# A hybrid attention, convolution and SwiGLU block: the order of the attention values' split, when V is copied, and where the last block's transposed products are read

## The chip, the cores and the metric

The kernel runs on one core of one Trainium2 chip. The metric is the device time of one execution in microseconds (us), the median of several runs. The profile is one further execution, recorded by the hardware profiler.

## The reference

One layer on x of 256 rows and 2048 columns, in float32, cut to what matters here:

```python
xn = rms_norm(h, norm1_g)
proj = xn @ w_in                                   # 2048 x 5120
q, k, v, ga, gg = split(proj)                      # 4 heads; q, k: 2 x 128 each, v: 256 each
att = diff_attention(rope(rms_norm(q)), rope(rms_norm(k)), v, lam)
att = rms_norm(att, subln_g) * (1 - lambda_init)   # over a head's 256 columns
u = silu(layer_norm(causal_depthwise_conv(ga * sigmoid(gg))))
h = h + concatenate([att, u]) @ w_out
hn = rms_norm(h, norm2_g)
h = h + (silu(hn @ w_gate) * (hn @ w_up)) @ w_down # 5632 hidden columns
```

In diff_attention each head has two score matrices; the weights are the first softmax less lam times the second.

## The kernel before, in words

**Products.** Every float32 product is made of three faster ones. A matrix is split into a rounded part (hi) and the residue (lo), and hi times hi, lo times hi and hi times lo are summed in PSUM. Weights come from HBM in chunks of two 128-row pieces of 512 columns (raw, L329); ScalarE rounds them (whi, L338), VectorE subtracts (wlo, L347). For some chunks ScalarE negates the raw chunk instead (lod, L333, or wlo, L341) and GpSimd's queue issues a DMA that adds the weights on top (L334, L342). The rounding runs three chunks ahead of the product before the FFN, four in it. The left operands are split in the same way and transposed: the pairs are called lhi and llo, and mahi and malo for attention heads 0 and 1.

**Order of the work.** Everything is written out by hand in one program order, engine by engine; what one engine needs of another becomes a wait on a semaphore. The main line is run_chunks (L470): for each chunk it issues loads, roundings and subtractions ahead, then the chunk's matmuls (multiply, L359). A chunk has a first half (hi times weights hi, L377, and lo times weights hi, L378) and a second half (hi times weights lo, L383). After each half multiply calls resume() (L250), which advances every side job by one step. Side jobs are Python generators: each issues some instructions and then yields; lag(n) yields n times, so that the job goes on n steps later. A step is thus half a chunk. In the FFN the same goes for units of a block (multiply_pair, multiply_two). Side jobs run in the order in which they were started.

**PSUM.** Of eight banks four are accumulators (acc) and four are shared by side jobs (aux). room(n) lets a job wait, while the program is written out, until fewer than five are held; a new tile takes a bank that earlier jobs have released in program order, and its first instruction waits until the last reader of that bank is done. Accesses to one bank by two engines are put in program order by waits.

**Attention.** For two heads at a time: attend_scores (L719) makes scores (ps_s, L728), masks and finds the maximum (L736, L738), takes exponentials (L747), reciprocals (L756), the product a with minus lam on GpSimd (L758), p (L767) and the weights (L774), transposes them (ps_wt, L780 to L782) and copies them to qT (L785). V comes from two blocks of w_in; when one has been multiplied, v_done (L788) copies it to SBUF with the row scale (L791) and starts attend_values (L797) for its two heads. That job multiplies (ps_o, L807), sums squares (L513 through L812), makes the scale on GpSimd (L216, L217), scales (att, L818), transposes (ps_at, L826), and splits the transposed tile into hi and lo (split_scaled, L236: L239 on ScalarE, L240 on VectorE), once for each half e of the head's columns. The pairs are columns 2*hd and 2*hd+1 of the left operand of w_out.

**Meanwhile.** VectorE works off the convolution's taps (y, L593), handed out between the halves of chunks by a credit. conv_back (L607) transposes the result (ps_y, L614), copies it (L619), takes the layer norm (L624, L633, L642), transposes back (ps_ln, L652) and applies Silu (L656). The chunks of w_out follow those of V: columns 0 to 3 of the left operand for three blocks n, then 4 and 5, then 6 and 7, then the convolution's.

**FFN.** The 5632 hidden columns are eleven blocks of 512, in groups of 4, 4 and 3. After a group, its part of w_down is multiplied. From the second block on, a part of the products is made by a scheme of seven products in place of eight (pair_sums, PRODUCTS; units "s"), the rest plainly (units "g" and "u"; L1106, L1107, L1111). block_done (L1201) combines a block's sums in tiles sum0 to sum3, and five steps later transposed (L936) takes the result in two halves t: transposes to PSUM (ps_a, L917), rounds (L948) and, three steps later, subtracts (L950). Where a half goes into the seven-product scheme, pair_forms (L954) is used, which first copies the PSUM tile to SBUF (L960). During a block all accumulators and three aux banks hold sums, so one bank is left for ps_a. For the last block, j = 10, both halves take the plain way.

Of the kernel before, what the change touches and what calls it, by code (L numbers as in the profile page):

```python
# [13 lines left out]
F32 = mybir.dt.float32  # L14
F32R = mybir.dt.float32r
AF = mybir.ActivationFunctionType
ALU = mybir.AluOpType
AX = mybir.AxisListType

P = 128  # L20
D = 2048
S = 256
# [8 lines left out]
FF = 5632  # L31
KD = D // P
N = 512
# [79 lines left out]
def tile_block(  # L113
# [6 lines left out]
    act, dve, pool, pe, sp = nc.scalar, nc.vector, nc.gpsimd, nc.tensor, nc.sync  # L120
# [6 lines left out]
    pre = prestack.enter_context(tc.tile_pool(name="pre", bufs=2))  # L127
# [37 lines left out]
    def col(key, k):  # L165
        return cols[:, AT[key] + k : AT[key] + k + 1]
# [45 lines left out]
    def rsqrt_mean(dst, ss, n, eps):  # L212

        k = dst.shape[-1]
        t = small.tile([P, 8], F32, tag="rsq", name="rsq")
        pool.tensor_scalar(t[:, :k], ss, 1.0 / n, eps, ALU.mult, ALU.add)  # L216
        pool.tensor_tensor(dst, t[:, :k], neghalf[:, :k], ALU.pow)  # L217
# [5 lines left out]
    def lhs_pair(pfx, k):  # L223
        if k % 2 == 0:
            halves[pfx] = lhs_two(pfx, k)
        return tuple(t[:, k % 2, :] for t in halves[pfx])

    def lhs_two(pfx, k):
        at = slot[0] % (KD // 2) * 4
        slot[0] += 1  # L230
        return arena_two(at)
# [4 lines left out]
    def split_scaled(pair, src, scale):  # L236

        hi, lo = pair
        act.activation(hi, src, AF.Copy, scale=scale)  # L239
        dve.scalar_tensor_tensor(lo, src, scale, hi.bitcast(F32), ALU.mult, ALU.subtract)  # L240
# [6 lines left out]
    def start(gen):  # L247
        running.append(gen)
# [6 lines left out]
    def lag(n):  # L255
        for _ in range(n):
            yield
# [4 lines left out]
    def room(n, hold=0):  # L262
        while held[0] + n > AUX:
            yield
        held[0] += hold
# [6 lines left out]
    def spend(us):  # L272
        credit[0] -= us
# [237 lines left out]
    def square_sum(src, accum, **kw):  # L511
        junk = pre.tile([P, N], F32, tag="junk", name="junk", bufs=1)
        act.activation(junk[:, : src.shape[-1]], src, AF.Square, accum_out=accum, **kw)  # L513
# [91 lines left out]
    mixa = {}  # L605
# [180 lines left out]
        wTs[hd] = wT  # L786

    def v_done(b, ps):  # L788
        yield
        for m in range(NM):  # L790
            act.activation(v_sb[m][:, b * N : (b + 1) * N], ps[m], AF.Copy, scale=rstd1[m])  # L791
        yield
        for hd in (2 * b, 2 * b + 1):
            start(attend_values(hd))
            yield

    def attend_values(hd):  # L797
        while hd not in wTs:
            yield
        wT = wTs.pop(hd)  # L800
        yield from lag(2)
        atts = []
        yield from room(1, 1)
        o = aux_ps.tile([P, NM, E], F32, tag="aux", name="ps_o")
        for m in range(NM):
            for k in range(m + 1):
                pe.matmul(o[:, m, :], wT[:, (0 if m == 0 else 1 + k), :], v_sb[k][:, hd * E : (hd + 1) * E],  # L807
                          start=k == 0, stop=k == m)
        yield
        ss = small.tile([P, NM], F32, tag="sso", name="sso")  # L810
        for m in range(NM):
            square_sum(o[:, m, :], ss[:, m : m + 1])  # L812
        r = small.tile([P, NM], F32, tag="ro", name="ro")
        rsqrt_mean(r, ss, E, EPS)
        yield from lag(2)
        for m in range(NM):
            at_ = pre.tile([P, E], F32, tag="att", name="att", bufs=4)
            act.activation(at_, o[:, m, :], AF.Copy, scale=r[:, m : m + 1])  # L818
            atts.append(at_)
        held[0] -= 1  # L820
        yield
        yield from room(1)
        pt = aux_ps.tile([P, 2, S], F32, tag="aux", name="ps_at")
        for e in range(2):
            for m in range(NM):
                pe.transpose(pt[:, e, m * P : (m + 1) * P], atts[m][:, e * P : (e + 1) * P], ident)  # L826
        for e in range(2):
            mixa[2 * hd + e] = lhs_pair("a", 2 * hd + e) if hd >= 2 else tuple(
                pre.tile([P, S], F32R, tag=t, name=t, bufs=4) for t in ("mahi", "malo"))
            split_scaled(mixa[2 * hd + e], pt[:, e, :], col("sg", e))  # L830
        spend(-0.9)


# [48 lines left out]
    ffn = {}  # L882
# [30 lines left out]
    def transpose_two(pt, aa, t):  # L913
        for i in range(2):
            for m in range(NM):
                c = (2 * t + i) * P
                pe.transpose(pt[:, i, m * P : (m + 1) * P], aa[m][:, c : c + P], ident)  # L917

    def group_of(j):
        return next((g for g in range(len(FGROUPS)) if j < sum(FGROUPS[: g + 1])), None)  # L920

    def place(g):

        pairs = DOWN[g]["pairs"]
        at = 7 * len(pairs)
        fhi, flo = (a[:, :at].rearrange("p (f q) c -> p f q c", f=7) for a in arena)
        twos = [(j, t) for j in range(sum(FGROUPS[:g]), sum(FGROUPS[: g + 1])) for t in range(2) if (j, t) not in pairs]
        free = [arena_two(i) for i in range(at, BLOCKS - 3, 4)]
        free += [tuple(a[:, i] for a in spare_lhs) for i in range(2)]
        assert len(free) >= len(twos)  # L930
        down[g] = dict(forms=(fhi, flo), pairs=pairs, twos=twos, at=dict(zip(twos, free)), ready=set())
# [4 lines left out]
    def transposed(j, aa):  # L936
        g = group_of(j)
        if g not in down:
            place(g)
        d = down[g]  # L940
        for t in range(N // P // 2):
            pt = aux_ps.tile([P, 2, S], F32, tag="aux", name="ps_a")
            transpose_two(pt, aa, t)
            if (j, t) in d["pairs"]:
                yield from pair_forms(j, t, pt)
            else:
                hi, lo = d["at"][j, t]
                act.copy(hi, pt)  # L948
                yield from lag(3)
                dve.tensor_tensor(lo, pt, hi.bitcast(F32), ALU.subtract)  # L950
            d["ready"].add((j, t))
            yield from lag(2)

    def pair_forms(j, t, pt):  # L954

        fp = ffn["pool"]
        q = down[group_of(j)]["pairs"].index((j, t))
        fhi, flo = (f[:, :, q] for f in down[group_of(j)]["forms"])
        a = fp.tile([P, 2, NM, P], F32, tag="sum0", name="af")
        act.copy(a, pt)  # L960
        a11, a21, a12, a22 = a[:, 0, 0], a[:, 0, 1], a[:, 1, 0], a[:, 1, 1]
        act.copy(fhi[:, :2], a[:, :, 0])
        act.activation(fhi[:, 2], a22, AF.Copy, scale=-1.0)
        yield from lag(2)
        f = fp.tile([P, 4, P], F32, tag="sum2", name="fs")
        dve.scalar_tensor_tensor(f[:, 1], a21, -1.0, a22, ALU.mult, ALU.subtract)
        dve.scalar_tensor_tensor(f[:, 2], f[:, 1], -1.0, a11, ALU.mult, ALU.subtract)
        dve.tensor_tensor(f[:, 3], a11, a21, ALU.subtract)
        dve.tensor_tensor(f[:, 0], a12, f[:, 2], ALU.subtract)
        dve.tensor_tensor(flo[:, :2], a[:, :, 0], fhi[:, :2].bitcast(F32), ALU.subtract)  # L970
        dve.scalar_tensor_tensor(flo[:, 2], a22, -1.0, fhi[:, 2].bitcast(F32), ALU.mult, ALU.subtract)
        yield from lag(2)
        act.copy(fhi[:, 3:], f)
        yield from lag(2)
        dve.tensor_tensor(flo[:, 3:], f, fhi[:, 3:].bitcast(F32), ALU.subtract)
# [225 lines left out]
    def block_done(j, q):  # L1201
        while "g" not in halfway:
            yield
        g, u = halfway.pop("g"), halfway.pop("u")
        for m, i in enumerate((Q3, QX)):
            dve.tensor_tensor(u[m], q[i], u[m], ALU.add)
        for m in range(NM):
            dve.tensor_tensor(u[m], u[m], g[m], ALU.mult)
        yield from lag(TO_TRANSPOSE)
        yield from transposed(j, u)  # L1210
# [51 lines left out]
    for b in range(2):  # L1262
        block("w_in", VC + b * N, range(KD), fx, lambda ps, b=b: v_done(b, ps))
# [66 lines left out]
```

## Time and profile before

| | us |
|---|---|
| median of 3 runs | 1044.78 |
| lowest and highest | 1044.53, 1044.81 |
| the profiled execution | 1043.19 |
| its span, first to last instruction | 1041.0 |
| TensorE busy | 1030.0 |
| VectorE busy | 864.5 |
| ScalarE busy | 685.1 |
| GpSimd busy | 157.4 |

The profiled execution's own time is 2.2 us more than its span, and 1.6 us less than the median. The granted TensorE clock was full throughout. The profile calls the engines PE (TensorE's matmuls; PEld its weight loads), DVE (VectorE), ACT (ScalarE), POOL (GpSimd) and SP. A row of the timeline gives start and duration in us, engine, line, operation, output and inputs, shape and count; idle time of the engine just before it stands in brackets, with what ended it. Matmuls overlap, so a row's duration is longer than the distance to the next matmul.

### The profile page before, as it was taken

What the parts mean: (1) busy time and instruction counts of PE and PEld (TensorE: products, weight loads), DVE (VectorE), ACT (ScalarE), POOL (GpSimd) and SP (SyncE); (2) the same over time, 40 slices, a digit from 0 to 9 for tenths busy, and PEclk for the clock granted to TensorE, in tenths of its full rate; (3) what the DMA queues carried; (4) which work ended last, traced back from release to release, by engine and by line L of the source; (5) the groups of instructions that cost most, each with busy time, mean ns of one, the idle gap of its engine ahead of it and who ended that gap; (6) DMA issues with size and microseconds to landing.
All of it is one profiled execution on the core that took longest, in us unless ns stands there. A gap on an engine that the chain in (4) does not pass through costs nothing.

```text
span 1041.0 us, 13235 instructions
## 1 busy us (share of the span) xinstructions
PE 1030.0 (99%) x4739; PEld 854.7 (82%) x4739; DVE 864.5 (83%) x1088; ACT 685.1 (66%) x865; POOL 157.4 (15%) x197
## 2 busy tenths in 40 slices
PE   8999999999999999999999999999999999999998
PEld 8888888887788888788888888888888888888786
DVE  5799989996546599999979689998896697998983
ACT  6855567857756567777656567776765666767661
POOL 0130134322110101011002120110101121001121
PEclk9999999999999999999999999999999999999999
DMA  9776867675566669898889998987979999889896
GB/s 361 277 205 227 258 184 205 197 206 155 188 182 233 227 217 284 232 328 241 260 238 294 269 308 265 306 236 245 303 201 270 306 272 327 236 249 301 241 252 134
DMA packets 65346, 258.06 MB, mean 248 GB/s; under 512 B 7424, under 2 KB 8448, under 8 KB 57856
## 3 DMA queue, kind: packets, MB, share of 16 engines
q1 hardware_dynamic: 48224, 201.34, 53.4%
q0 software_dynamic: 16768, 55.58, 28.0%
q8 instruction: 37, 0.61, 0.2%
q10 hardware_dynamic: 288, 0.29, 0.1%
q14 instruction: 29, 0.24, 0.1%
HBM read 248.80 MB, written 8.39 MB: 247 GB/s over the span
## 4 chain that ended last, share of the span: by engine, by line
PE 94%; ACT 2%; DVE 1%; issue 1%; DMA 1%; POOL 1%; SPq 0%; DVEq 0%; ACTq 0%
PE q L1106 11%; PE q L1107 11%; PE q L1111 11%; PE acc L383 11%; PE acc L378 11%; PE acc L377 11%; PE q L1085 9%; PE q L1087 8%; PE q L1086 8%; PE ps_a L917 1%; DMA raw<-in_wts_dram 1%; ACT whi L338 1%; PE ps_s L728 1%; PE ps_h L854 0%; PE ps_qk L713 0%
## 5 line engine op out<-in xcount | busy, mean ns | idle before, releaser
L338 ACT CAST whi<-raw 128x1024 fp32r<-128x1024 f32 (+1 forms) x261 | 270.7, 1045 | 105.7 <-PE acc L378 46.3
L347 DVE TENSOR_TENSOR wlo<-raw,whi 128x1024 fp32r<-128x1024 f32 (+1 forms) x173 | 209.4, 1216 | 76.5 <-ACT whi L338 76.5
L377 PE MATMUL acc<-whi,lhi 128*128 128x512 f32 (+1 forms) x448 | 167.4, 379 | 1.6 <-ACT whi L338 1.2
L378 PE MATMUL acc<-whi,llo 128*128 128x512 f32 (+1 forms) x448 | 165.7, 375 | 0.9 <-DVE llo L240 0.9
L1068 DVE TENSOR_TENSOR wl<-wt,wh 128x2048 fp32r<-128x2048 f32 x58 | 132.6, 2287 | 20.1 <-ACT wh L1063 20.1
L1059 ACT CAST wh<-wb 128x1536 fp32r<-128x1536 f32 x58 | 86.0, 1483 | 87.1 <-PE q L1086 42.8
L342 POOL DMA_DIRECT2D wlo<-in_wts_dram x74 | 65.0, 889 | 510.7 <-ACT wlo L341 482.6
L1106 PE MATMUL q<-whi,chi 128*128 128x512 f32 x320 | 124.7, 390 | 0.0
L1107 PE MATMUL q<-whi,clo 128*128 128x512 f32 x320 | 124.6, 389 | 0.0
L1063 ACT CAST wh<-wt 128x2048 fp32r<-128x2048 f32 x58 | 110.4, 1904 | 18.6 <-DVE wt L1054 18.6
L1085 PE MATMUL q<-wh,fhi 128*128 128x512 f32 x280 | 109.1, 390 | 0.4 <-DVE sum L1190 0.4
L1087 PE MATMUL q<-wl,fhi 128*128 128x512 f32 x280 | 109.0, 389 | 0.0
L1086 PE MATMUL q<-wh,flo 128*128 128x512 f32 x280 | 108.9, 389 | 0.0
L1067 DVE TENSOR_TENSOR wl<-wb,wh 128x1536 fp32r<-128x1536 f32 x58 | 101.6, 1751 | 2.1 <-ACT wh L1059 2.1
L593 DVE SCALAR_TENSOR_TENSOR y<-upad,cw,y 128x256 f32<-128x256 f32 x240 | 101.9, 484 | 0.6 <-ACT y L586 0.4
L383 PE MATMUL acc<-wlo,lhi 128*128 128x512 f32 (+1 forms) x404 | 101.9, 377 | 0.0
L377 PEld LDWEIGHTS acc<-whi,lhi 128*128 128x128 f32 x448 | 84.4, 188 | 17.1 <-ACT whi L338 1.6
L378 PEld LDWEIGHTS acc<-whi,llo 128*128 128x128 f32 x448 | 84.4, 188 | 16.0 <-DVE llo L240 1.1
L1111 PE MATMUL q<-wlo,chi 128*128 128x512 f32 x320 | 86.9, 393 | 0.0
L383 PEld LDWEIGHTS acc<-wlo,lhi 128*128 128x128 f32 x404 | 71.5, 189 | 12.7
L341 ACT ACTIVATE wlo<-raw 128x1024 fp32r<-128x1024 f32 x74 | 78.1, 1056 | 0.0
L1052 DVE TENSOR_TENSOR wt<-wb 128x1024 f32<-128x1024 f32 x58 | 70.8, 1220 | 0.8 <-DMA wb<-in_wts_dram 0.4
(216 smaller groups left out, 1733.1 us busy)
## 6 DMA issues: line engine op xcount, KB each, us to landing
raw<-in_wts_dram SPq DMA_DIRECT2D x259, 512.0 KB, 5.8
wb<-in_wts_dram SPq DMA_DIRECT2D x57, 1024.0 KB, 8.1
wlo<-in_wts_dram POOLq DMA_DIRECT2D x74, 512.0 KB, 9.5
lod<-in_wts_dram POOLq DMA_DIRECT2D x14, 512.0 KB, 6.9
out_dram<-sum POOLq DMA_DIRECT2D x22, 256.0 KB, 7.0
h<-in_x_dram SPq DMA_DIRECT2D x4, 512.0 KB, 9.5
out_dram<-h POOLq DMA_DIRECT2D x8, 256.0 KB, 3.7
xt<-in_xt_dram SPq DMA_DIRECT2D x3, 512.0 KB, 7.3
```

The source lines that it names most:

```text
L338: act.copy(c["hi"], c["raw"])
L347: dve.tensor_tensor(c["lo"], c["raw"], c["hi"].bitcast(F32), ALU.subtract)
L377: pe.matmul(ps[m], xhi[:, ms], hi[:, j, :], start=c["first"] and j == 0, stop=False)
L378: pe.matmul(ps[m], xlo[:, ms], hi[:, j, :], start=False, stop=False)
L383: pe.matmul(ps[m], xhi[:, ms], lo[:, j, :], start=False, stop=c["last"] and j == nk - 1)
L1068: dve.tensor_tensor(c["lo"][:, :4], c["t"], c["hi"][:, :4].bitcast(F32), ALU.subtract)
L1085: pe.matmul(ps, fhi[:, f, p, :], c["hi"][:, w], start=bool(first), stop=False)
L1086: pe.matmul(ps, flo[:, f, p, :], c["hi"][:, w], start=False, stop=False)
L1087: pe.matmul(ps, fhi[:, f, p, :], c["lo"][:, w], start=False, stop=bool(last))
L1106: pe.matmul(ps, plain[i][0][:, ms], hi[:, i, :], start=i == 0 and bool(c["first"].get(qs[m])), stop=False)
L1107: pe.matmul(ps, plain[i][1][:, ms], hi[:, i, :], start=False, stop=False)
L1111: pe.matmul(sum_bank(c, qs[m]), plain[i][0][:, ms], lo[:, i, :], start=False, stop=i == 1 and bool(c["last"].get(qs[m])))
```

## The change

Four edits:

1. v_done no longer waits a step: V is copied at the first resume() after its last chunk, and the values of its heads start one step earlier.
2. attend_values waits two steps in place of one between scaling and transposes.
3. The two roundings of a head are issued one after the other, and then the two residues.
4. In the last block ScalarE first copies each half's transposed products from PSUM to an SBUF tile, and rounding and residue read that tile. It takes the place of sum0 (t = 0) or sum2 (t = 1), whose contents were used up by the product of gate and up values before.

```diff
     def v_done(b, ps):
-        yield
         for m in range(NM):
             act.activation(v_sb[m][:, b * N : (b + 1) * N], ps[m], AF.Copy, scale=rstd1[m])
...
         held[0] -= 1
-        yield
+        yield from lag(2)
         yield from room(1)
...
-        for e in range(2):
-            mixa[2 * hd + e] = lhs_pair("a", 2 * hd + e) if hd >= 2 else tuple(
-                pre.tile([P, S], F32R, tag=t, name=t, bufs=4) for t in ("mahi", "malo"))
-            split_scaled(mixa[2 * hd + e], pt[:, e, :], col("sg", e))
+        pairs = [lhs_pair("a", 2 * hd + e) if hd >= 2 else tuple(
+            pre.tile([P, S], F32R, tag=t, name=t, bufs=4) for t in ("mahi", "malo")) for e in range(2)]
+        for e, (hi, _) in enumerate(pairs):
+            act.activation(hi, pt[:, e, :], AF.Copy, scale=col("sg", e))
+        for e, (hi, lo) in enumerate(pairs):
+            dve.scalar_tensor_tensor(lo, pt[:, e, :], col("sg", e), hi.bitcast(F32), ALU.mult, ALU.subtract)
+            mixa[2 * hd + e] = hi, lo
...
                 hi, lo = d["at"][j, t]
+                if j == FF // N - 1:
+                    a = ffn["pool"].tile([P, 2, S], F32, tag=f"sum{2 * t}", name="ac")
+                    act.copy(a, pt)
+                    pt = a
                 act.copy(hi, pt)
                 yield from lag(3)
                 dve.tensor_tensor(lo, pt, hi.bitcast(F32), ALU.subtract)
```

## The prediction

> **What bounds the kernel now.** I read the page first, then TensorE's waits over the whole run, then the timeline of the two places that the diff touches.
>
> ```profile
> span 1041.0 us, 13235 instructions
> ...
> PE 1030.0 (99%) x4739; PEld 854.7 (82%) x4739; DVE 864.5 (83%) x1088; ACT 685.1 (66%) x865; POOL 157.4 (15%) x197
> ...
> PE 94%; ACT 2%; DVE 1%; issue 1%; DMA 1%; POOL 1%; SPq 0%; DVEq 0%; ACTq 0%
> ```
>
> TensorE is busy for 99% and makes 94% of the chain that ended last. A change outside its queue can only shorten the moments in which it stands still. The longest line of its waits in the touched code, and the only one between the two touched places:
>
> ```profile
> PE ps_a L917 <- DVE llo L950: 1.1, 1, 1.1
> ...
> PE q L1085 <- DVE sum L1190: 0.4, 1, 0.4
> ```
>
> The columns are total, count and longest, in us. The touched code has five more short ones, which the timeline places. Since matmuls are pipelined, a stall is longer than the idle time shown: 512-column matmuls start 0.23 us apart, so I measure it from the previous start plus 0.23 to the next start.
>
> **Attention values: the stalls.** The timeline from 224 to 268 us (start, duration, engine, line; in brackets idle time before it and what ended that):
>
> ```profile
> 238.00 0.67 PE L826 MATMUL ps_at<-ident,att 128*128 128x128 f32 x4 [0.35 <-DVE malo L240]
> ...
> 242.04 0.47 DVE L240 SCALAR_TENSOR_TENSOR malo<-ps_at,cols,mahi 128x256 fp32r<-128x256 f32 x1
> ...
> 242.55 0.48 ACT L239 ACTIVATE mahi<-ps_at,cols 128x256 fp32r<-128x256 f32 x1 [3.17 <-DVE malo L240]
> ...
> 243.06 0.48 DVE L240 SCALAR_TENSOR_TENSOR malo<-ps_at,cols,mahi 128x256 fp32r<-128x256 f32 x1 [0.55 <-ACT mahi L239]
> ...
> 245.56 0.77 PE L614 MATMUL ps_y<-ident,y 128*128 128x128 f32 x5 [0.17 <-DVE y L593]
> ...
> 247.35 2.34 DVE L347 TENSOR_TENSOR wlo<-raw,whi 128x1024 fp32r<-128x1024 f32 x2
> ...
> 247.45 2.43 POOL L758 TENSOR_TENSOR a<-r,neg_lam 128x1 f32<-128x1 f32 x2 [13.73 <-DVE r L756]
> ...
> 251.09 1.07 PE L383 MATMUL acc<-wlo,mahi 128*128 128x512 f32 x4
> ...
> 251.42 0.49 ACT L785 COPY qT<-ps_wt 128x384 f32<-128x384 f32 x1
> ...
> 251.79 1.29 ACT L791 ACTIVATE v<-acc,rstd 128x512 f32<-128x512 f32 x2
> ...
> 252.55 0.50 PE L377 MATMUL acc<-whi,mahi 128*128 128x512 f32 x1 [0.40 <-ACT v L791]
> ...
> 260.01 0.47 ACT L785 COPY qT<-ps_wt 128x384 f32<-128x384 f32 x1
> ...
> 261.53 1.28 PEld L807 LDWEIGHTS ps_o<-v,qT 128*128 128x128 f32 x6
> ...
> 261.81 0.36 ACT L513 ACTIVATE junk<-ps_o 128x256 f32<-128x256 f32 x1
> ...
> 262.86 1.27 PE L383 MATMUL acc<-wlo,mahi 128*128 128x512 f32 x4
> ...
> 263.85 0.84 ACT L818 ACTIVATE att<-ps_o,ro 128x256 f32<-128x256 f32 x2
> ...
> 264.75 0.66 PE L826 MATMUL ps_at<-ident,att 128*128 128x128 f32 x4 [0.62 <-ACT att L818]
> ...
> 265.44 0.48 ACT L239 ACTIVATE lhi<-ps_at,cols 128x256 fp32r<-128x256 f32 x1 [0.75 <-PE ps_at L826]
> ...
> 266.98 0.48 DVE L240 SCALAR_TENSOR_TENSOR llo<-ps_at,cols,lhi 128x256 fp32r<-128x256 f32 x1 [0.55 <-ACT lhi L239]
> ...
> 267.61 0.63 PE L652 MATMUL ps_ln<-ident,upad 128*128 128x128 f32 x4 [0.37 <-DVE llo L240]
> ```
>
> Stalls: at 252.55 the last of four matmuls before it began at 251.09 + 1.07 - 0.39 = 251.77, 0.23 more is 252.00, so 0.55 us. At 264.75 likewise from 263.97, 0.78. Both exceed the idle time shown by 0.15, so I put the others at that much more than theirs: 0.50 at 238.00, 0.32 at 245.56, 0.52 at 267.61. Sum 2.7 us.
>
> The row at 242.55 shows the mechanism. Both rounds (ScalarE) and both residues (VectorE) read one PSUM bank, and accesses to a bank from two engines are put in order as they are issued. So the second rounding waits for the first residue, which is queued on VectorE behind convolution work: ScalarE loses 3.17 us, VectorE then 0.55.
>
> **Attention values, part by part.** A step is half a chunk, one call of resume.
>
> *Rounding order (L827 to L830).* Each engine's own order stays; four alternations become one. Four instructions of 0.48 still follow each other, but two by two, and a pair back to back takes 0.84 (the scalings at 263.85). From the first rounding to the end of the last residue it is 266.98 + 0.48 - 265.44 = 2.02 now, and 2 x 0.84 with one handoff, about 1.8, after. For head 1 the second residue ends 0.2 + 0.6 = 0.8 us earlier on VectorE, which is packed there, so the last convolution tap before 245.56 is earlier by that.
>
> *V copies half a chunk earlier (L789).* On ScalarE they stay behind the same weight roundings but pass the qT copy of 0.49 at 251.42, so each ends about 0.37 earlier (starts 251.42 and 251.79). Heads 0 to 2 get product, squares and scaling half a chunk earlier; the lag of 2 puts their transposes back where they were. Head 3 waits for its qT copy, so its transposes move half a chunk later, and so do its residues:
>
> ```profile
> 274.49 0.48 DVE L240 SCALAR_TENSOR_TENSOR llo<-ps_at,cols,lhi 128x256 fp32r<-128x256 f32 x1 [0.54 <-ACT lhi L239]
> ...
> 279.03 0.39 PE L377 MATMUL acc<-whi,lhi 128*128 128x512 f32 x1
> ```
>
> The last residue now ends at 274.97 and the w_out chunk that reads it starts at 279.03: half a chunk is about 1.4 us, so 4.1 us of cover hide it; beyond that every us late is a us of TensorE.
>
> *Head 1, 238.00.* Its scaled values now precede head 0's rounding by half a chunk, and a bank freed earlier is at hand. The 0.50 goes.
>
> *What is added there.* The products of heads 0 and 1 move ahead of, and behind, a chunk's second half; the negation queued on ScalarE waits for that half:
>
> ```profile
> 225.78 1.46 PE L807 MATMUL ps_o<-v,qT 128*128 128x256 f32 x6
> ...
> 225.98 1.06 ACT L333 ACTIVATE lod<-raw 128x1024 fp32r<-128x1024 f32 x1 [3.94 <-PE acc L383]
> ...
> 229.89 0.49 ACT L747 ACTIVATE pr<-ps_s,nmx 128x256 f32<-128x256 f32 x1
> ...
> 231.12 1.48 PE L728 MATMUL ps_s<-kT,qT 128*128 128x128 f32 x8
> ```
>
> Head 0's product takes 1.1 us of TensorE (1.46 less the overlap), so the negation starts near 227.5 behind head 0's squares, and head 2's exponentials, which now also stand behind head 1's squares, end at 229.89 + 0.49 + 1.6 = 231.95 or so. Head 3's scores take their banks: the second bank is wanted 0.86 after 231.12, at 231.98. Cost 0 to 0.3 us; I take 0.1. TensorE is then 0.4 ahead, VectorE 0.7, and at 245.56 TensorE resumes with VectorE: 0.7 ahead.
>
> *GpSimd's a, 247.45.* The first of its two tiny products ends only with the two VectorE subtractions around it. It moves with VectorE: 0.7. ScalarE's p, copies and V copies follow: V is 0.7 + 0.37 = 1.07 earlier. TensorE would be ready at 252.00 - 0.70 = 251.30 and gets V at 252.55 - 1.07 = 251.48: **1.07 ahead**.
>
> *Heads 2 and 3, 260 to 268.* Head 2's two squares with their accumulator reads (0.36 for the first, about 0.95 in all) now stand ahead of the qT copy at 260.01, which so comes at 260.01 + 0.95 less what ScalarE is ahead: 0.7 if all of its chain has moved, 0.3 (an estimate) if the layer norm's GpSimd steps in between have not. It ends at 260.7 to 261.1. Head 3's product, at 261.53 now, would be due at 261.53 - 1.07 = 260.46 and waits for it: TensorE falls back to 0.4 to 0.7 ahead. Then head 2's scaling, no longer behind a weight rounding, is done before its transposes are due: they start at 263.97 - (0.4 to 0.7), which is 1.2 to 1.5 before 264.75. From 264.75 to 267.61 it was 2.86, which the rounding order shortens by 0.2: **1.4 to 1.7 us ahead, 1.5 taken**. Ends of the range: 0.5 (only the stall at 238.00) and 2.7 (all).
>
> The Trainium skill bears on the GpSimd row: "SBUF — State Buffer", Who interferes with whom, says that a VectorE instruction with two SBUF inputs and a GpSimd instruction that reads SBUF exclude each other, and the blocked one goes on when the other ends. Here the trace agrees only in part: the wait outlasted the first subtraction. By that rule alone GpSimd would go on after one subtraction, the first rival below, and the sum would come to 2.6 us instead of 1.8.
>
> **Last block's products copied.** The timeline from 970 to 1000 us:
>
> ```profile
> 983.77 0.58 ACT L948 CAST lhi<-ps_a 128x512 fp32r<-128x512 f32 x1
> ...
> 986.12 0.39 PE L1087 MATMUL q<-wl,lhi 128*128 128x512 f32 x1
> ...
> 987.58 0.66 PE L917 MATMUL ps_a<-ident,sum 128*128 128x128 f32 x4 [1.07 <-DVE llo L950]
> ...
> 988.27 0.59 ACT L948 CAST lhi<-ps_a 128x512 fp32r<-128x512 f32 x1 [2.01 <-PE ps_a L917]
> ...
> 988.30 0.39 PE L1107 MATMUL q<-whi,llo 128*128 128x512 f32 x1
> ...
> 990.03 0.68 DVE L950 TENSOR_TENSOR llo<-ps_a,lhi 128x512 fp32r<-128x512 f32 x1
> ...
> 991.06 0.39 PE L1107 MATMUL q<-whi,llo 128*128 128x512 f32 x1
> ```
>
> The same cast from SBUF, in the groups by line of 880 to 1000 us (count, busy us, mean ns, idle before):
>
> ```profile
> L973 ACT CAST lhi<-fs 128x512 fp32r<-128x512 f32 x3 | 1.8, 609 | 0.0
> ```
>
> The stall is 987.58 - 986.12 - 0.23 = 1.23 us: the second transposes need the one free bank, held until VectorE's residue. The change adds two copies of about 0.58 on ScalarE and takes the roundings from SBUF at 0.61; the bank is free at 984.4. ScalarE was idle for 2.0 us before its second rounding, which covers this. So the transposes start at 986.35. But the residue stays where VectorE's queue has it: the first matmul that needs it cannot pass 987.58 (was 988.30, 0.72 gained), and the second residue, ending at 990.71, holds the next at 990.77 (was 991.06). The wait moves from the bank to the data: **0.3 us** is left, ends 0 and 0.7.
>
> **Sum.** 1.5 + 0.3 = 1.8 us. TensorE's waits list shows only one other from 285 us on, 0.4 us for a VectorE sum, so nothing later gives it back. The profiled execution took 1043.19 (span 1041.0 plus 2.2 around it): 1041.4 after. It lies 1.6 below the median; from the median, 1044.78 - 1.8 = **1043.0**, that is 0.17%. About 0.2%, 2.1 us, can be told from no change.
>
> **Rivals.**
> 1. *GpSimd slips in between the two subtractions* (1.2 us sooner than I count). For it: the handover between two subtractions could let it in; against it: 247.45 lasted through both. Then V is never waited for (0.70 + 0.55 = 1.25 ahead), nor head 3's copy, nor head 2's scaling (+0.78), and 0.23 at the banks: 2.3 + 0.3 = 2.6 us, 1042.2. Chance 0.2.
> 2. *The gain stops at the ScalarE chain*: GpSimd's lock does not move with VectorE, and head 2's squares push head 3's copy. For it: the chain around 244 to 261 is ScalarE's and GpSimd's. Then 0.3 of 0.37 and the 0.3 at the end: 0.6 us, 1044.2. Chance 0.2.
> 3. *Slower: the exponentials behind the moved squares.* At 231.12 head 3's scores wait one for one once the exponentials end after 231.98. If the moved negation and squares cost 2 us more than counted, TensorE loses 2.0; the stall at 238.00 and the 0.7 on VectorE give back 1.2, the rest runs on through GpSimd and V: +0.8 - 0.3, 1045.3. Against it: ScalarE idles 3.94 us just before. Chance 0.07.
>
> **How the numbers follow.** Forecast 0.53, over 1.3 to 2.3 us. The range 1041.9 to 1044.9 takes in rival 2 and most of rival 1. Faster by over 0.2%: nearly all of rival 1 and a quarter of the forecast, 0.33; slower 0.04; the rest, 0.63, within 0.2%.
>
> **What would show it.** After: no ScalarE wait on malo or llo of L240; no stall of L826; V copies ahead of the qT copy near 251; a wait of L1107 for llo at 987 in place of that of L917. I am wrong if a stall at L728 near 231 appears, if L807 waits over 0.5 us for qT, or if L758 ends early.

## The result, and the profile after

| | before | after |
|---|---|---|
| median of 11 runs, us | 1044.81 | 1041.82 |
| lowest and highest, us | 1043.69, 1045.41 | 1041.50, 1043.94 |
| the profiled execution, us | 1043.19 | 1041.78 |
| its span, us | 1041.0 | 1039.6 |

The ratio of the runs is 0.9978, with a 95% interval from 0.9970 to 0.9986. On the 1044.78 that the prediction started from that is 1044.78 x 0.9978 = 1042.5 us, 2.3 us less, with an interval of 1.5 to 3.1. The change made the kernel faster, by 0.22%, which lies just at the bound of 0.2% that the prediction set; the interval reaches to both sides of it. After's own median, 1041.82, lies 0.08 under the low end of the forecast range, 1041.9.

In the code after, the lines have new numbers: V copy L790, values product L806, scaling L817, transposes L825, roundings L829, residues L831; in the last block transposes L919, copy L952, rounding L954, residue L956, matmuls L1112, L1113 and L1117.

The page of after, in the same lines as before:

```profile
span 1039.6 us, 13246 instructions
...
PE 1031.3 (99%) x4739; PEld 856.1 (82%) x4739; DVE 863.9 (83%) x1088; ACT 686.5 (66%) x867; POOL 152.6 (15%) x197
...
PE 96%; ACT 1%; issue 1%; DVE 1%; DMA 1%; SPq 0%; DVEq 0%
```

TensorE's share of the chain that ended last rose from 94% to 96%: the work is the same, there is less standing still. TensorE's waits over the whole run of after (total, count, longest, in us):

```profile
PE acc L377 <- ACT whi L338: 1.6, 1, 1.6
PE ps_warm L147 <- POOL neghalf L141: 1.4, 1, 1.4
PE q L1113 <- DVE llo L956: 0.6, 2, 0.4
PE q L1091 <- DVE sum L1196: 0.4, 1, 0.4
PE acc L378 <- DVE llo L240: 0.4, 1, 0.4
```

The 1.1 us for the bank of the last block's transposes is gone; two waits for the residue itself stand in its place, as forecast. The waits for the attention's malo and for its scaled values are gone as well. (The first, second and last line belong to the first 13 us.)

**A measure without the first 204 us.** The median and the profiled execution of before differ by 1.6 us, and in after they do not (1041.82 and 1041.78). To compare traces I therefore take the stretch from the last weight-residue matmul before the attention (the 301st L383, near 204 us) to the start of the last pair of matmuls. Its two ends, in the timeline of before:

```profile
203.50 0.39 PE L383 MATMUL acc<-wlo,lhi 128*128 128x512 f32 x1
...
1036.62 0.61 PE L1111 MATMUL q<-wlo,lhi 128*128 128x512 f32 x2
```

and of after:

```profile
204.03 0.39 PE L383 MATMUL acc<-wlo,lhi 128*128 128x512 f32 x1
...
1035.21 0.61 PE L1117 MATMUL q<-wlo,lhi 128*128 128x512 f32 x2
```

The rows differ by 833.12 and 831.18; with the 0.23 from the first to the second matmul of the pair the stretch is 833.35 before and 831.41 after: **1.94 us shorter**. After began the stretch 0.53 later. In what follows a *lead* is a time of before, less the time of after, plus 0.53.

**Attention values in after.** The timeline from 231 to 268 us:

```profile
231.73 0.49 ACT L747 ACTIVATE pr<-ps_s,nmx 128x256 f32<-128x256 f32 x1
...
232.36 0.73 PEld L728 LDWEIGHTS ps_s<-kT,qT 128*128 128x128 f32 x4 [0.26 <-ACT pr L747]
...
233.18 0.34 POOL L758 TENSOR_TENSOR a<-r,neg_lam 128x1 f32<-128x1 f32 x2 [1.11 <-DVE r L756]
...
238.38 0.60 PE L825 MATMUL ps_at<-ident,att 128*128 128x128 f32 x4
...
239.01 0.84 ACT L829 ACTIVATE mahi<-ps_at,cols 128x256 fp32r<-128x256 f32 x2 [0.51 <-PE ps_at L825]
...
242.65 0.87 DVE L831 SCALAR_TENSOR_TENSOR malo<-ps_at,cols,mahi 128x256 fp32r<-128x256 f32 x2
...
246.06 0.48 PE L377 MATMUL acc<-whi,mahi 128*128 128x512 f32 x1
...
247.32 2.34 DVE L347 TENSOR_TENSOR wlo<-raw,whi 128x1024 fp32r<-128x1024 f32 x2
...
247.43 2.43 POOL L758 TENSOR_TENSOR a<-r,neg_lam 128x1 f32<-128x1 f32 x2 [13.91 <-DVE r L756]
...
249.75 0.80 ACT L767 ACTIVATE p<-pr,a 128x128 f32<-128x128 f32 x2 [4.15 <-POOL a L758]
...
251.40 1.28 ACT L790 ACTIVATE v<-acc,rstd 128x512 f32<-128x512 f32 x2
...
252.15 0.50 PE L377 MATMUL acc<-whi,mahi 128*128 128x512 f32 x1
...
252.55 0.49 ACT L785 COPY qT<-ps_wt 128x384 f32<-128x384 f32 x1
...
261.39 1.16 PEld L806 LDWEIGHTS ps_o<-v,qT 128*128 128x128 f32 x6 [0.27 <-ACT qT L785]
...
262.60 1.28 PE L383 MATMUL acc<-wlo,mahi 128*128 128x512 f32 x4
...
263.72 0.60 PE L825 MATMUL ps_at<-ident,att 128*128 128x128 f32 x4
...
265.23 0.88 DVE L831 SCALAR_TENSOR_TENSOR llo<-ps_at,cols,lhi 128x256 fp32r<-128x256 f32 x2 [6.56 <-ACT lhi L829]
...
266.25 0.63 PE L652 MATMUL ps_ln<-ident,upad 128*128 128x128 f32 x4
```

The roundings at 239.01 and the residues at 242.65 now come as pairs of 0.84 and 0.87, and neither second one waits. ScalarE's 3.17 us for the residue are gone; but ScalarE then stands for 4.15 us at 249.75 for GpSimd's a, where it stood 1.61 before:

```profile
249.77 0.81 ACT L767 ACTIVATE p<-pr,a 128x128 f32<-128x128 f32 x2 [1.61 <-POOL a L758]
```

The time that the new order gave ScalarE was passed on to a wait that GpSimd ends. The transposes at 238.38 and 263.72 start without a stall, and the V copies at 251.40 precede the qT copy at 252.55. There are two new waits: at 232.36 for an exponential, and at 261.39, where the weight load of head 3's product waits 0.27 for the qT copy.

**The last block in after.** The timeline from 982 to 990 us:

```profile
982.48 0.57 ACT L952 COPY ac<-ps_a 128x512 f32<-128x512 f32 x1
...
983.09 0.62 ACT L954 CAST lhi<-ac 128x512 fp32r<-128x512 f32 x1
...
985.07 0.60 PE L919 MATMUL ps_a<-ident,sum 128*128 128x128 f32 x4
...
985.55 0.68 DVE L956 TENSOR_TENSOR llo<-ac,lhi 128x512 fp32r<-128x512 f32 x1
...
986.29 0.50 PE L1113 MATMUL q<-whi,llo 128*128 128x512 f32 x1 [0.39 <-DVE llo L956]
986.62 0.40 PE L1112 MATMUL q<-whi,lhi 128*128 128x512 f32 x1
...
988.74 0.69 DVE L956 TENSOR_TENSOR llo<-ac,lhi 128x512 fp32r<-128x512 f32 x1
...
989.48 0.50 PE L1113 MATMUL q<-whi,llo 128*128 128x512 f32 x1 [0.18 <-DVE llo L956]
989.82 0.40 PE L1112 MATMUL q<-whi,lhi 128*128 128x512 f32 x1
```

The second transposes at 985.07 don't wait for a bank. The first L1113 does: the matmul before it started at 985.42, so 986.29 - 985.42 - 0.23 = 0.64 us. The second loses 0.34 in the same measure (by the distance to the matmul before it).

### The profile page after: what moved, and what is told of

The parts are those of the page before. It is cut to its first block, busy times and chain, and to the rows that moved or that the text cites. A ratio compares the mean times of both kernels' runs of the same rounds, so it can differ in the third digit from the quotient of the medians.

```text
span 1039.6 us, 13246 instructions
## 1 busy us (share of the span) xinstructions
PE 1031.3 (99%) x4739; PEld 856.1 (82%) x4739; DVE 863.9 (83%) x1088; ACT 686.5 (66%) x867; POOL 152.6 (15%) x197
## 4 chain that ended last, share of the span: by engine, by line
PE 96%; ACT 1%; issue 1%; DVE 1%; DMA 1%; SPq 0%; DVEq 0%
PE q L1113 11%; PE q L1117 11%; PE q L1112 11%; PE acc L377 11%; PE acc L378 11%; PE acc L383 11%; PE q L1091 9%; PE q L1093 8%; PE q L1092 8%; PE ps_a L919 1%; DMA raw<-in_wts_dram 1%; PE ps_s L728 0%; PE ps_o L806 0%; PE ps_qk L713 0%; PE ps_h L856 0%
## 5 line engine op out<-in xcount | busy, mean ns | idle before, releaser
L377 PE MATMUL acc<-whi,lhi 128*128 128x512 f32 (+1 forms) x448 | 168.3, 380 | 1.6 <-ACT whi L338 1.6
L1112 PE MATMUL q<-whi,chi 128*128 128x512 f32 x320 | 124.7, 390 | 0.0
L1113 PE MATMUL q<-whi,clo 128*128 128x512 f32 x320 | 124.6, 389 | 0.0
L383 PE MATMUL acc<-wlo,lhi 128*128 128x512 f32 (+1 forms) x404 | 102.1, 378 | 0.0
L377 PEld LDWEIGHTS acc<-whi,lhi 128*128 128x128 f32 x448 | 85.2, 190 | 16.8 <-ACT whi L338 2.0
L1117 PE MATMUL q<-wlo,chi 128*128 128x512 f32 x320 | 86.9, 393 | 0.0
L383 PEld LDWEIGHTS acc<-wlo,lhi 128*128 128x128 f32 x404 | 71.9, 190 | 12.7
```

The source lines that it names most:

```text
L377: pe.matmul(ps[m], xhi[:, ms], hi[:, j, :], start=c["first"] and j == 0, stop=False)
L383: pe.matmul(ps[m], xhi[:, ms], lo[:, j, :], start=False, stop=c["last"] and j == nk - 1)
L1112: pe.matmul(ps, plain[i][0][:, ms], hi[:, i, :], start=i == 0 and bool(c["first"].get(qs[m])), stop=False)
L1113: pe.matmul(ps, plain[i][1][:, ms], hi[:, i, :], start=False, stop=False)
L1117: pe.matmul(sum_bank(c, qs[m]), plain[i][0][:, ms], lo[:, i, :], start=False, stop=i == 1 and bool(c["last"].get(qs[m])))
```

## Experiments

Eight kernels. The first four ran beside one another, the last four likewise on another chip, each beside runs of the kernel before. All times of the table are from the profiled executions, one for each kernel, in us. "To 320" is from the start of the stretch to the 448th L377, in the products of w_out (320.43 in before); "320 to 936" goes from there to the 4291st matmul of the program (935.60 in before); "936 on" is the rest, with both transposes of the last block. Both borders are set by the number of the matmul, so that the same work is compared.

| kernel | ratio to before, 95% interval | to 320 | 320 to 936 | 936 on | stretch |
|---|---|---|---|---|---|
| before | | 116.92 | 615.18 | 101.25 | 833.35 |
| after | 0.9978 (0.9970 to 0.9986) | 115.09 | 615.20 | 101.13 | 831.41 |
| e1 before again | 1.0000 (0.9991 to 1.0008) | 116.94 | 615.19 | 101.22 | 833.35 |
| e2 rounding order only | 0.9983 (0.9974 to 0.9992) | 115.75 | 615.17 | 101.23 | 832.14 |
| e3 V early, lag 2 only | 0.9997 (0.9988 to 1.0006) | 116.25 | 615.19 | 101.23 | 832.67 |
| e4 copy only | 0.9998 (0.9989 to 1.0007) | 116.91 | 615.19 | 101.07 | 833.16 |
| e5 after, a on VectorE | 0.9974 (0.9964 to 0.9985) | 114.47 | 615.39 | 101.09 | 830.95 |
| e6 after, last residues earlier | 0.9968 (0.9956 to 0.9979) | 115.11 | 615.21 | 100.60 | 830.91 |
| e7 after, lag 1 | 0.9995 (0.9986 to 1.0004) | 116.51 | 615.19 | 101.12 | 832.82 |
| e8 e5 and e6 | 0.9963 (0.9950 to 0.9975) | 114.51 | 615.18 | 100.57 | 830.25 |

The ratios of e3, e4 and e7 are not clear of 1; what is said of these three rests on the stretch alone. The column "936 on" shows how far such numbers hold: 101.22 to 101.25 in the four without the copy (before, e1, e2, e3), 101.07 to 101.13 in the four with it and nothing else changed there (after, e4, e5, e7).

The theory that the experiments test: the time came from the attention values, mostly through the order of roundings and residues, and a little from the last block; the difference between the medians that goes beyond 1.9 us is not the change's. The rivals stand with each expectation.

### e1: the kernel before, once more

No edit.

> The kernel before, once more, to learn how far two executions of one program lie apart. Theory A (the change took away stalls worth about 2 us; the profile of before was a fast execution): ratio 1.000 within 0.1%, and a span 0.5 to 1.5 us longer than 1041.0, most of it before the first weight matmuls. Theory C (the profile of before is typical and the change is worth only its 1.4 us of span): span 1041.0 within 0.3 us.

The median was 1043.90 us beside 1043.86 for its reference runs, and the profiled execution took 1044.64, where that of before took 1043.19. The timeline of e1, with the ends of the stretch:

```profile
68.70 1.21 PE L383 MATMUL acc<-lod,lhi 128*128 128x512 f32 x4 [1.09 <-DMA lod<-in_wts_dram]
...
204.95 0.39 PE L383 MATMUL acc<-wlo,lhi 128*128 128x512 f32 x1
...
1038.07 0.61 PE L1111 MATMUL q<-wlo,lhi 128*128 128x512 f32 x2
```

The stretch is 833.35, to 0.01 us that of the first profile. All of the 1.45 us lies before it, and 1.25 of it at one place: at 68.70 TensorE waited for one DMA of weights. The profile of before has no wait there:

```profile
67.43 1.07 PE L383 MATMUL acc<-lod,lhi 128*128 128x512 f32 x4
```

The same wait, of 1.0 to 2.1 us from start to start, stands in the profiles of e2, e3, e4 and e8, and in none of after, e5, e6 and e7. The code there is the same in all. So the profiled execution of before was one without this wait, and an execution grows by 1 to 2 us with this one arrival. The span, 1042.4, is in theory A's range; where I had looked for the time, ahead of the first weight matmuls, was wrong. Whether the wait comes equally often in both kernels was not counted. Nor is it all that moves ahead of the stretch: e5 began the stretch at 205.28, 1.78 later than before, without this wait; the clock granted to TensorE from 11 to 16 us was 0.66 there, and 1.00 in before.

### e2: the rounding order alone

```diff
-        for e in range(2):
-            mixa[2 * hd + e] = lhs_pair("a", 2 * hd + e) if hd >= 2 else tuple(
...
-            split_scaled(mixa[2 * hd + e], pt[:, e, :], col("sg", e))
+        for e, (hi, _) in enumerate(pairs):
+            act.activation(hi, pt[:, e, :], AF.Copy, scale=col("sg", e))
+        for e, (hi, lo) in enumerate(pairs):
+            dve.scalar_tensor_tensor(lo, pt[:, e, :], col("sg", e), hi.bitcast(F32), ALU.mult, ALU.subtract)
```

> Only the order of roundings and residues (edit 3). Theory A (each part removes its own stalls): ScalarE no longer waits at 242.5 for a residue, VectorE is 0.7 us ahead before the convolution's transposes, the stall of L826 at 238.0 is gone or halved, V and what follows come 0.7 earlier; the stalls at V (0.55) and at head 2's scaling (0.78) stay; total 0.7 to 1.2 us, ratio 0.9988 to 0.9994. Theory B (ScalarE's 3.17 us wait is the cause of all later stalls): all of the attention's gain, 1.9 us, ratio 0.998.

Measured: 1.21 us less in the stretch, 1.17 of it up to 320; the ratio alone is clear of 1 as well. At 0.9983 it lies below the theory's 0.9988 to 0.9994 and nearer to the rival's 0.998; its interval holds both, so the ratio cannot part them. The timeline of e2:

```profile
239.75 0.87 ACT L830 ACTIVATE mahi<-ps_at,cols 128x256 fp32r<-128x256 f32 x2
...
250.39 0.80 ACT L767 ACTIVATE p<-pr,a 128x128 f32<-128x128 f32 x2 [4.14 <-POOL a L758]
...
253.17 0.50 PE L377 MATMUL acc<-whi,mahi 128*128 128x512 f32 x1 [0.41 <-ACT v L791]
```

This one edit takes the stalls at 238 and at the convolution's transposes, but V stays late (0.57 us from start to start) and so do head 2's scaled values (0.6 idle): these two need the other edits. It is the largest part, as the theory said; the rival, that it is all of the gain, is out by these two stalls and by 1.17 against after's 1.83 up to 320.

### e3: V early and the lag of 2 alone

```diff
     def v_done(b, ps):
-        yield
...
-        yield
+        yield from lag(2)
```

> Only V one step earlier and the transposes one step later (edits 1 and 2). Theory A: the stalls at 238.0 (0.5), V (0.4) and head 2's scaling (0.5 to 0.8) go, minus 0.3 at head 3's scores behind the exponentials; ScalarE's wait of about 3 us for a residue stays; total 0.8 to 1.3 us, ratio 0.9988 to 0.9993. Theory B: under 0.3 us or slower, ratio 0.9997 to 1.0005.

Measured: 0.68 us, under the 0.8 to 1.3 that I had expected and over the rival's 0.3. The timeline of e3:

```profile
245.18 0.47 ACT L239 ACTIVATE mahi<-ps_at,cols 128x256 fp32r<-128x256 f32 x1 [3.90 <-DVE malo L240]
...
248.18 0.65 PE L614 MATMUL ps_y<-ident,y 128*128 128x128 f32 x4 [0.73 <-DVE y L593]
```

The stalls at 238 and at the scaling are gone, and of that at V 0.17 us is left. But with the old order of roundings the second one still waits for the first residue, and VectorE's last convolution tap comes so late that the stall at its transposes grows from 0.34 to 0.90 us. An earlier step only moves TensorE into the next late engine. The parts add: 1.21 + 0.68 + 0.19 (below) = 2.08, together 1.94.

### e4: the copy alone

```diff
+                if j == FF // N - 1:
+                    a = ffn["pool"].tile([P, 2, S], F32, tag=f"sum{2 * t}", name="ac")
+                    act.copy(a, pt)
+                    pt = a
```

> Only the last block's copy (edit 4). Theory A (the wait moves from the bank to the residue in VectorE's queue): the stall of L917 (1.22 us) becomes two of the second matmul's residue, about 0.6 and 0.35; 0.3 us, ratio 0.9997. Rival: the whole 1.2 us, ratio 0.9988.

Measured: 0.19 us in the stretch, 0.18 of it from 936 on. TensorE's waits in e4:

```profile
PE q L1111 <- DVE llo L954: 0.5, 2, 0.4
```

The wait for the bank (1.23 us from start to start) became two waits for the residue (0.62 and 0.34). The bank was one of two things that were late; the copy frees only that.

### e5: GpSimd's product on VectorE

```diff
-            pool.tensor_tensor(a1, r[:, 1:2], neg_lam, ALU.mult)
+            dve.tensor_tensor(a1, r[:, 1:2], neg_lam, ALU.mult)
```

> The changed kernel with the tiny product a (L758) made by VectorE right behind the reciprocals instead of by GpSimd. Measured from the 301st weight residue matmul (L383, near 204 us) to the last matmul: the kernel before 833.35 us in two executions, the changed one 831.41. Theory A (GpSimd is locked out by the two subtractions and holds ScalarE for 4.1 us at 249.75; only the small stalls left at V, at head 3's product and at the banks hang on that): ScalarE's p near 247.5, these stalls go, 0.3 to 0.6 us less, 830.8 to 831.1. Rival (my prediction's first rival, all of ScalarE's lateness is GpSimd's): over 0.6 us less. Third possibility: same, because what follows V waits for the layer norm on GpSimd anyway.

Measured: 0.62 us less than after up to 320, just over the 0.3 to 0.6 expected, and 0.46 in the whole stretch. The rival began at 0.6, and e8, with the same edit, has 0.58; the size alone does not part the two. The timeline of e5:

```profile
248.63 0.16 DVE L758 TENSOR_TENSOR a<-r,neg_lam 128x1 f32<-128x1 f32 x1
...
248.88 0.81 ACT L767 ACTIVATE p<-pr,a 128x128 f32<-128x128 f32 x2 [2.04 <-DVE r L756]
...
248.98 2.36 DVE L347 TENSOR_TENSOR wlo<-raw,whi 128x1024 fp32r<-128x1024 f32 x2
```

The product takes 0.16 us, and p starts before the pair of subtractions that it had to outlast in after. The stalls at V (in after the matmul at 252.15 still came 0.19 late, and two behind it about 0.11 each) and at head 3's product are gone; they make 0.42 and 0.14 us of the 0.62, so the gain is where the theory had put it. The 0.20 that this trace lost between 320 and 936 did not come back in e8, which has the same edit, so it is not put down to it.

### e6: the last block's residues two units earlier

```diff
-                yield from lag(3)
+                yield from lag(1 if j == FF // N - 1 else 3)
```

> The changed kernel with one step in place of three between rounding and residue in the last block. If the gain of the copy is used up by the residue's place in VectorE's queue, both stalls of L1113 (0.64 and 0.34 us) go; VectorE stands about 2 us waiting for the rounding and its large subtractions come 2.7 us later, which is covered by its 2.6 us of idle time near 997. 0.7 to 1.0 us less, stretch 830.4 to 830.7. Rival: the later subtractions hold TensorE at the next seven-product unit, no gain or slower.

Measured: 0.50 us less than after in the stretch, 0.53 of it from 936 on, under the 0.7 to 1.0 expected. The timeline of e6:

```profile
983.88 0.69 DVE L956 TENSOR_TENSOR llo<-ac,lhi 128x512 fp32r<-128x512 f32 x1 [1.97 <-ACT lhi L954]
...
986.16 2.29 DVE L1074 TENSOR_TENSOR wl<-wt,wh 128x2048 fp32r<-128x2048 f32 x1
...
988.36 0.68 DVE L956 TENSOR_TENSOR llo<-ac,lhi 128x512 fp32r<-128x512 f32 x1
...
989.10 0.50 PE L1113 MATMUL q<-whi,llo 128*128 128x512 f32 x1 [0.16 <-DVE llo L956]
```

The first residue is done at 984.57, and the first stall of 0.64 is gone, though VectorE now idles 1.97 us for the rounding. The second residue still stands behind a subtraction of 2.29 us, so its stall stays, 0.33. I had counted on both.

### e7: without the longer lag

```diff
-        yield from lag(2)
+        yield
```

> The changed kernel with the single step between scaling and transposes put back: V early, but transposes early too. Theory A (the second step gives the scaled values time): for heads 0 and 1 nothing is lost, their values are ready 1 us ahead; head 2's transposes come half a chunk earlier, near 260.5, while its values are ready at 263.5: a stall of 2 to 3 us, of which the present wait at head 3's product gives back little; stretch 1 to 2.5 us longer, 832.4 to 833.9. Rival (the lag is not needed): 831.4 or less.

Measured: 1.41 us longer than after. The timeline of e7:

```profile
237.17 0.66 PE L825 MATMUL ps_at<-ident,att 128*128 128x128 f32 x4 [0.73 <-ACT att L817]
...
262.62 0.91 PE L825 MATMUL ps_at<-ident,att 128*128 128x128 f32 x4 [0.94 <-ACT att L817]
```

The transposes now come a step earlier and wait for their scaled values, 0.89 us at 237 and 1.36 at 262 from start to start. The total was as expected, its parts were not: head 2's stall was put at 2 to 3 us, and the first pair of heads was to lose nothing. So the lag is what makes the early V copy pay: without it the stage up to 320 takes 116.51 us, more than the 115.75 of e2, which has the new order of roundings but V as late as before.

### e8: e5 and e6 together

> The two edits of e5 and e6 together on the changed kernel. Theory A (stalls far apart add): the sum of the two gains, 1.0 to 1.6 us less than the changed kernel, stretch 829.8 to 830.4; against the kernel before a ratio of 0.9965 to 0.9975.

Measured: a stretch of 830.25, 1.16 less than after, which is 0.46 + 0.50 and the 0.20 that e5's trace had lost. The stretch is inside the range expected, the ratio, 0.9963, just under its 0.9965 to 0.9975: 0.37% under before, with a median of 1040.60 us. That it is faster than after rests on the stretch, since the intervals of the two ratios overlap.

## Why the prediction was right, and where its sizes were off

The total came as argued: 1.8 us forecast, 1.94 in the stretch, and a ratio that gives 2.3 with an interval of 1.5 to 3.1. The experiments put the gain where the prediction put it. That the total lies so near is in part luck: up to 320 us the gain was 0.33 more than the 1.5 taken, and in the last block 0.18 less than the 0.3. By the prediction's own steps, with leads from the rows:

- **The stall at 238.00 goes: right**, in after, e2 and e3.
- **Exponentials behind moved squares, 0 to 0.3, 0.1 taken: mis-sized.** The transposes of head 1 lead by 238.00 - 238.38 + 0.53 = 0.15, where 0.50 less 0.1 was forecast; so the cost was 0.35, just over its upper end. The exponential that frees the second bank ended at 232.22, 231.69 on before's clock, earlier than the 231.95 forecast. (The prediction's own sum for it, 229.89 + 0.49 + 1.6, gives 231.98, not 231.95.) What failed is the time at which the bank was wanted: the second bank's weights were due to load at 232.36 - 0.26 = 232.10, 231.57 on before's clock, not 231.98. In before too the fifth of the eight matmuls, the first of the second bank, starts at 231.57, 0.45 after the first and not 0.86. A stall at L728 near 231 was one of the signs that the prediction had named for being wrong; the other two, a wait of over 0.5 us for qT and an early end of L758, did not come.
- **TensorE 0.7 ahead at the convolution's transposes: mis-sized by the same step.** Before resumed the weights here in this row of its timeline:

```profile
246.08 0.47 PE L377 MATMUL acc<-whi,mahi 128*128 128x512 f32 x1
```

  After did at 246.06, a lead of 0.55. VectorE was ready, as forecast (there is no wait for y); TensorE itself was the late one.
- **GpSimd's a moves with VectorE: right, by 0.55 in place of 0.7** (247.45 - 247.43 + 0.53), the value of the step before. **V 0.37 more for passing the qT copy: right to the hundredth** (251.79 - 251.40 + 0.53 = 0.92). TensorE leads by 0.93 at 252.15, forecast 1.07.
- **Head 3's product falls back to 0.4 to 0.7: right in mechanism, the fall too large.** Its weight load waits 0.27 for the qT copy and leads by 261.53 - 261.39 + 0.53 = 0.67. But in before that load ran 0.22 ahead of its matmul (261.53 and 261.75), and that margin takes up most of the wait: the matmuls behind the product lead by 262.86 - 262.60 + 0.53 = 0.79, 0.14 less than at V. ScalarE had moved whole, the better of the two cases considered.
- **Head 2's transposes 1.2 to 1.5, L652 1.4 to 1.7: right and a little short.** Leads are 264.75 - 263.72 + 0.53 = 1.56 and 267.61 - 266.25 + 0.53 = 1.89. The 0.79 and the stall of 0.78 that is gone make 1.57 for the first; from there to L652 the order of roundings gave 0.33, not the 0.2 counted. Up to 320 us 1.83 is left, where 1.5 was taken.
- **Last block 0.3, ends 0 and 0.7: right in mechanism, short in size.** The stage from 936 on is 0.12 shorter in after and 0.18 in e4 (0.02 to 0.03 of such a number is noise, by e1). The residue stayed the next late thing, as the step said. Inside this stage before runs 935.60 - 934.31 = 1.29 later than after; on before's clock the two stalled matmuls start at 987.58 and 990.77, both where the prediction had put them, and the second is so 0.29 earlier. What the step left out is that the matmul behind a stalled one starts 0.34 after it (986.62 after 986.29, 989.82 after 989.48), where 0.23 is usual: 0.11 more behind the second leaves 0.18. e6 shows the residue's place as the cause of the first stall.
- **The base: wrong as a figure.** The profiled execution was taken to lie 1.6 under the median in both kernels. In e1 the profiled execution was 1.45 longer, 1.25 of it at one arrival of a DMA near 69 us; that the runs at before's median had the same wait is likely but not shown. The forecast for the profiled execution, 1041.4, came out at 1041.78; after began the stretch 0.53 late, by what happened in its first 13 us.

Rival 1 (GpSimd slips in between two subtractions) did not happen in after: 247.43 + 2.43 outlasted both subtractions, 247.32 + 2.34, and e2 shows p waiting 4.14 in the same way. The rule that the prediction named, from the Trainium skill, "SBUF — State Buffer", Who interferes with whom (the blocked engine goes on when the other ends), is so not borne out as far as one instruction goes; that the two engines exclude each other agrees with these rows. What the rival would have been worth was tried in e5 by another way, without GpSimd: 0.62 us, where the prediction's sums differ by 0.8 in the attention. Rival 2 (the gain stops at ScalarE's chain, 0.6) is excluded by the 1.83. Rival 3's mechanism did appear, as the stall at 232.36, but at 0.35 and not at 2 us.

Open stays how the difference of the medians, 3.0 us, divides between the change and what moves ahead of the stretch; the ratio's interval holds the 1.94. It stays open too where after loses the last 0.06 us of the last block's 0.18, which e4 keeps.

## What to carry to other kernels

Where two engines alternate on one PSUM bank, issue each engine's accesses together: here four alternations turned into one were worth 1.2 us, because each handoff waits for what else is queued on the other engine. Moving a step earlier pays only if the steps that read its result have time too (e3 loses at the convolution's taps, e7 at the scaled values), so ask at each place which engine is late next. Measure a change of a few tenths of a per cent on the stretch that it touches, between two fixed matmuls, since whole times carry the arrivals of transfers that it doesn't touch.

## What the runs showed of the hardware

A product of 128 x 1 elements on GpSimd was held through two back-to-back VectorE subtractions: two of them took 2.43 us at 247.43, and 0.34 us at 233.18 of the same execution, with no subtraction beside them. On VectorE one took 0.16 us. How many instructions such a product is held through is not worked out: in the same trace of after two took 1.43 us at 184.69, the first held through three VectorE instructions, and 1.94 us at 192.52, where the first ended with a subtraction (near 194.06 and 194.02) although a tap followed at once (193.94). And the stretch of 833 us repeated to 0.01 us in two executions of one kernel, while their whole times differed by 1.45 us; e5's trace has 0.20 us between 320 and 936 that its edit does not explain, so one trace alone does not always hold to 0.01.
